# The two layer ends of a hybrid diffusion kernel: result parts by half in one page, places made earlier, sums of squares as columns on TensorE, root and reciprocal ahead of the loop

## The chip, the cores and the metric

One Trainium2 chip, one of its cores. The time is device microseconds of one execution of the whole program; each kernel is run several times, and the median of the runs stands for it.

## The reference

Two layers over 512 token columns (256 of them latent, 256 context) of 1024 channels. Each layer normalises and modulates, mixes with three parts (an S5 scan, an attention with low-rank queries and keys, a Hyena convolution), projects the merged result back, and ends with a mixture of 32 experts of which each token takes two. The second layer needs the latent columns alone. What the change touches is the mixture and the normalisation behind it:

```python
def _rms_norm(x, g):
    xf = x.astype(jnp.float32)
    y = xf * lax.rsqrt(jnp.mean(xf * xf, axis=-1, keepdims=True) + EPS)
    return (y * g.astype(jnp.float32)).astype(x.dtype)

def expert_block(args):                     # inside _hier_moe
    xb, e = args
    return (jax.nn.silu(xb @ w1[e]) * (xb @ w3[e])) @ w2[e]

for i in range(DEPTH):                      # inside reference
    hl = _modulate(xl, norm1_g[i], mod_l[0], mod_l[1])
    ...
    xl = xl + mod_l[2] * (_merge_groups(s5_l, mla_l, hy_l, mix_norm_g[i]) @ w_out[i])
    ...
    y = _hier_moe(fl, moe_w_group[i], moe_w_expert[i], moe_w1[i], moe_w3[i], moe_w2[i])
    xl = xl + mod_l[5] * y.reshape(bsz, n, d)
return _rms_norm(xl, final_g)
```

## The kernel before

The program runs `mixer(0)`, `moe(0)`, `mixer(1)`, `moe(1)` and a final stage (`FIN`), in this order. `xT` holds the running result as eight channel tiles of 128 channels by 512 columns. Weights come in pages of 128x1024 float32 (512 KB) out of a ring of 44 pages, and every one of these transfers is issued by SP, one after another in one fixed order: a page whose place in the ring isn't free yet holds SP until it is, and all that stands behind it in SP's order waits too.

Two things set the order. In `mixer` a scheduler lays out the instructions of every engine by a simulated timeline; in `moe` the order is the written one. Whatever is written between the two calls belongs to the scheduled part.

**The end of `mixer(1)`.** After the last head of the attention (the exponentials on ScalarE, `ACT`, then line 1111 on VectorE, `DVE`, which scales by the reciprocal of the sums in `ATTst`) the output projection (line 1373) runs over eight output tiles m = 0 to 7. Each takes one page of `in_wout`, which ScalarE and VectorE split into a high and a low part first. Pages 0 to 2 are loaded ahead (names `ATTpg<-in_wout`), pages 3 to 7 later (`OUTpg<-in_wout`). Between the two groups SP issues eight pages of the modulation weights (`ADApg<-in_adaw`, used by line 166) and the first 16 expert pages (`ROUTpg<-in_w`). The router follows, then the experts.

**`moe`.** Each of the 32 experts takes twelve pages: eight in `first_half` (line 1582, `pC`, `pY`, `pT` and the like are PSUM banks), then `swiglu`, `turn` (transposes into `hT`), and four in `second_half` (line 1606). `scaled_result` weights the 128 x 512 result, by two halves of 64 rows, and splits it: ScalarE writes the high part into the page `Y[0]`, VectorE (line 1718) the rest into `Y[1]`. A pair of experts shares the 128 rows of these pages. `combine` then spreads the rows back over the columns by a matmul with the 0/1 matrix of places `GT` (lines 1790 and 1868 make it), channel tile by channel tile, and `residual` (line 1620) adds the eight tiles into `xT`. The combines of pair p run during the experts of pair p + 1; those of the last pair stand in `combine_last` (line 1698), where the squares of each finished tile are added up on VectorE (lines 193 and 1709). Layer 0 has one more expert pass, with weights chosen by a register, ahead of `combine_last`. A loop (line 1900) for overfull experts follows; here it runs zero times.

**Behind the loop**, `rstd_of` sums the squares over the channels by matmuls with a column pair of ones (line 201), takes the root on ScalarE (line 118, which needs a table load) and the reciprocal on VectorE (line 205), and spreads it over the partitions by transposes (line 217). In layer 0 this is the start of `mixer(1)`, where four weight pages are split as well (`S5bpg`) before the normalised input is made (line 224, `INPpg`); in layer 1 it is the final stage, which loads the gains `fg` (line 1953, 4 KB) and multiplies (line 1956).

## Time and profile before

| | us |
|---|---|
| runs | 1714.05, 1712.85, 1707.95 |
| median | 1712.85 |
| profiled execution | 1709.9 |
| its span | 1708.1 |
| TensorE busy | 1533.8 (90%) |
| VectorE busy | 888.6 (52%) |
| ScalarE busy | 482.4 (28%) |
| bytes moved | 510.04 MB, mean 299 GB/s |

Some 1.8 us of the profiled execution lie outside its span. Busy shares are means over stages with different limits; which wait ends last in a stage is read from that stage alone.

### The profile page before, as it was taken

The numbers are of one execution on the slowest core, as the hardware profiler recorded it, in microseconds if no ns is written. First come the engines' busy times: TensorE is split into PE (matmuls) and PEld (weight loads), VectorE is DVE, ScalarE is ACT, GpSimd is POOL, SyncE is SP. The second block draws the span as 40 slices with busy tenths as digits, with TensorE's granted clock in tenths as the row PEclk, the third lists the DMA queues.
The fourth block names the chain that finished last, engine by engine and source line by source line (L and its number), as shares of the span: only waits on it lengthen the run. The fifth ranks groups of instructions, "written<-read, shape, count | busy, mean of one in ns | idle before, by whom it ended". The sixth has DMA issues, their size and how long they took to land. (4 is left out here: it accounts for less than half of the span.)

```text
span 1708.1 us, 22533 instructions
## 1 busy us (share of the span) xinstructions
PE 1533.8 (90%) x8073; PEld 788.0 (46%) x8073; DVE 888.6 (52%) x2176; ACT 482.4 (28%) x931; POOL 94.7 (6%) x154
## 2 busy tenths in 40 slices
PE   5888889998999999999899597899799999999995
PEld 1676744476433333344233387547534444333322
DVE  6769565545244546864643758455524434333333
ACT  3343544342111121112122534444311111111112
POOL 0000212003000000002000000010100000000000
PEclk9998899998999999999999698998899999999998
DMA  9111244559999999999999112577799999999994
GB/s 343 64 38 62 79 181 162 218 198 351 374 392 407 409 409 409 409 408 372 373 402 409 61 62 99 205 264 267 293 359 409 409 409 409 409 409 409 409 409 184
DMA packets 143300, 510.04 MB, mean 299 GB/s; under 512 B 17995, under 2 KB 18573, under 8 KB 142929
## 3 DMA queue, kind: packets, MB, share of 16 engines
q1 hardware_dynamic: 138736, 495.21, 75.0%
q0 software_dynamic: 4160, 12.82, 2.2%
q8 instruction: 66, 1.08, 0.3%
q10 hardware_dynamic: 288, 0.52, 0.1%
q14 instruction: 50, 0.40, 0.1%
HBM read 504.85 MB, written 3.64 MB: 298 GB/s over the span
## 5 line engine op out<-in xcount | busy, mean ns | idle before, releaser
L1582 PE MATMUL MOEp<-MOEpg,MOEpg 128*64 128x512 f32 x956 | 227.4, 603 | 13.1 <-DMA MOEpg<-in_w 11.9
L1582 PE MATMUL MOEp<-MOEpg,ROUTpg 128*64 128x512 f32 x960 | 220.5, 603 | 8.2 <-DMA MOEpg<-in_w 7.9
L1718 DVE SCALAR_TENSOR_TENSOR MOEpg<-MOEpY,MOEwt,MOEpg 64x512 fp32r<-64x512 f32 x128 | 96.0, 750 | 241.5 <-ACT MOEpg L118 241.4
L1606 PE MATMUL MOEpY<-MOEpg,MOEhT 128*64 128x512 f32 x960 | 219.4, 599 | 1.8 <-DVE MOEhT L1598 1.8
L1620 DVE SCALAR_TENSOR_TENSOR zxT<-MOEpC,zmod,zxT 128x256 f32<-128x256 f32 x385 | 168.2, 479 | 8.2 <-PE MOEpC L1698 2.1
L118 ACT ACTIVATE MOEpg<-MOEpY,MOEwt 64x512 fp32r<-64x512 f32 x128 | 87.3, 682 | 276.3 <-PE MOEpY L1606 212.2
L1588 DVE TENSOR_TENSOR MOEh<-MOEh,MOEp 128x256 f32<-128x256 f32 x65 | 27.3, 420 | 241.9 <-ACT MOEh L118 241.9
L118 ACT ACTIVATE MOEh<-MOEp 128x256 f32<-128x256 f32 x65 | 24.9, 383 | 399.7 <-PE MOEp L1582 399.7
L1688 PE MATMUL MOEpC<-MOEGT,MOEpg 128*128 128x512 f32 (+1 forms) x496 | 130.0, 364 | 6.7 <-DVE zxT L1620 6.0
L1582 PEld LDWEIGHTS MOEp<-MOEpg,ROUTpg 128*64 128x64 f32 x960 | 64.2, 137 | 149.4 <-issue 103.7
L1582 PEld LDWEIGHTS MOEp<-MOEpg,MOEpg 128*64 128x64 f32 x956 | 59.4, 136 | 159.3 <-DMA MOEpg<-in_w 90.5
L1606 PEld LDWEIGHTS MOEpY<-MOEpg,MOEhT 128*64 128x64 f32 x960 | 63.5, 136 | 120.6 <-issue 93.8
L1688 PEld LDWEIGHTS MOEpC<-MOEGT,MOEpg 128*128 128x128 f32 x496 | 75.2, 189 | 61.7 <-issue 26.8
L166 PE MATMUL ADAb<-ADApg,zcact 128*32 128x512 f32 x384 | 76.1, 614 | 12.8 <-DMA ADApg<-in_adaw 12.8
L788 PE MATMUL PROJb<-INPpg,PROJpg 128*128 128x512 f32 (+1 forms) x384 | 73.8, 356 | 6.4 <-DVE PROJpg L974 5.7
L788 PEld LDWEIGHTS PROJb<-INPpg,PROJpg 128*128 128x128 f32 x384 | 63.5, 206 | 15.9 <-ACT PROJpg L118 6.7
L118 ACT ACT_TABLE_LOAD x35 | 44.9, 1283 | 15.7 <-DVE ATTst L1102 5.7
L1657 PE MATMUL MOEpG<-MOEpg,ROUTpg 128*128 128x256 f32 x240 | 44.7, 310 | 1.1 <-DVE MOEpg L1493 1.1
L1657 PEld LDWEIGHTS MOEpG<-MOEpg,ROUTpg 128*128 128x128 f32 x240 | 33.0, 194 | 24.2 <-issue 15.8
L1091 PE MATMUL ATTb<-QKVpg,QKVpg 96*128 96x512 f32 x64 | 35.4, 654 | 7.3 <-ACT ATTpg L118 7.3
L1373 PE MATMUL OUTb<-OUTpg,ATTpg 128*128 128x512 f32 (+1 forms) x192 | 41.3, 380 | 0.0
L1373 PEld LDWEIGHTS OUTb<-OUTpg,ATTpg 128*128 128x128 f32 x192 | 34.9, 214 | 5.3 <-DVE ATTpg L230 0.2
(541 smaller groups left out, 2115.2 us busy)
## 6 DMA issues: line engine op xcount, KB each, us to landing
MOEpg<-in_w SPq DMA_DIRECT2D x719, 512.0 KB
ADApg<-in_adaw SPq DMA_DIRECT2D x96, 512.0 KB
ROUTpg<-in_w SPq DMA_DIRECT2D x61, 512.0 KB
PROJpg<-in_win SPq DMA_DIRECT2D x16, 512.0 KB
ATTpg<-in_wout SPq DMA_DIRECT2D x8, 512.0 KB
OUTpg<-in_wout SPq DMA_DIRECT2D x8, 512.0 KB
QKVpg<-in_uq SPq DMA_DIRECT2D x5, 512.0 KB
MOEpg<-in_win SPq DMA_DIRECT2D x5, 512.0 KB
```

What stands on the lines that cost most here:

```text
L118: nc.scalar.activation(out, in_, f, **kw)
L166: nc.tensor.matmul(b[q:q + 32, :], cact[:, k, :], w[:, h * 512:(h + 1) * 512], start=(k < 2), stop=(k >= KD - 2), tile_position=(0, q))
L788: nc.tensor.matmul(b, a_[:, c], b_[k][:, c0:], start=(first and n == 0), stop=(last and n == 2))
L1091: nc.tensor.matmul(b, qc[h][:, nq - NS + qt * 128:nq - NS + (qt + 1) * 128], kc[h], start=True, stop=True)
L1373: nc.tensor.matmul(b, a_[:, c], y_, start=(n == 0 and j == 0), stop=(n == KD - 1 and j == 2))
L1582: nc.tensor.matmul(b[64 * h:64 * h + 64, :], X[:, k, :], w[:, h * 512:(h + 1) * 512], start=(k == 0), stop=(k == KD - 1), tile_position=(0 ...
L1588: nc.vector.tensor_mul(h_, h_, b[:, 256:512])
L1606: nc.tensor.matmul(b[64 * h:64 * h + 64, :], hT[:, k % 2, (k // 2) * 64:(k // 2) * 64 + 64], w[:, h * 512:(h + 1) * 512], start=(k == 0), ...
L1620: nc.vector.scalar_tensor_tensor(xT[:, k, seg(s)], b[:, s * NS - c0:(s + 1) * NS - c0], mod[:, 40 + k, s:s + 1], xT[:, k, seg(s)], op0=OP. ...
L1657: nc.tensor.matmul(b[:, kk * 256:(kk + 1) * 256], hs[t][:, k * 128:(k + 1) * 128], G[:, t].rearrange("p e c -> p (e c)"), start=(t == 0 an ...
L1688: nc.tensor.matmul(b, Y_[p][j][rows, k * 128:(k + 1) * 128], GT_[p][rows], start=(j == 0), stop=(j == 1))
L1718: nc.vector.scalar_tensor_tensor(Y[1][rows_of, h * 512:(h + 1) * 512], b[rows], wt[rows], yh.bitcast(F32), op0=OP.mult, op1=OP.subtract)
```

## The change

- `scaled_result` puts both parts of one half of the result in one page (`Y[h]`: high in columns 0 to 511, low in 512 to 1023), and `combine` reads them there through `part_of`.
- `GT` is made ahead of `second_half` instead of behind `scaled_result`; likewise in the extra pass (`extra_places`).
- In layer 1's last expert the four combines that used to stand around `turn` and behind the result now stand inside `first_half`, one ahead of each second page.
- `combine_last` hands the squares to TensorE as column sums (`sum_columns`) while it still combines: three sums in layer 0 (tiles 0 to 5, 6, 7) and five in layer 1 (0+1, 2+3, 4+5, 6, 7). Root and reciprocal (`rstd_from`) come ahead of the loop, and only the spreading (`spread`) behind it.
- The loop's own ring of pages has two instead of four.
- `fg` is loaded between `mixer(1)` and `moe(1)`, in a pool that is opened there and stays open; the final products go into two pages.

```diff
+        for j, sq in enumerate(acc):
+            sum_columns(sq, n, b, j == 0, j == len(acc) - 1)
+        return rstd_from(b, nch, n)
+
+    def sum_columns(sq, n, b, first, last):
+
         nt = n // 128
-        for j, sq in enumerate(acc):
-            for t in range(nt):
-                nc.tensor.matmul(b[:, 2 * t:2 * t + 2], sq[:, t * 128:(t + 1) * 128], ones2,
-                                 start=(j == 0 and t == 0), stop=(j == len(acc) - 1 and t == nt - 1))
-        r = cpool.tile([128, 4], F32, name=uid("rs"), tag="rs", bufs=4)
+        for t in range(nt):
+            nc.tensor.matmul(b[:, 2 * t:2 * t + 2], sq[:, t * 128:(t + 1) * 128], ones2,
+                             start=(first and t == 0), stop=(last and t == nt - 1))
+
+    def rstd_from(b, nch, n, r=None):
+        nt = n // 128
+        if r is None:
+            r = cpool.tile([128, 4], F32, name=uid("rs"), tag="rs", bufs=4)
...
-            rstd1 = rstd_of(None, D, acc=acc)
+            rstd1 = spread(acc, NT)
...
+        def part_of(p, j, k):
+            return Y_[p][k // 4][:, j * 512 + k % 4 * 128:j * 512 + (k % 4 + 1) * 128]
+
         def combine_last(p, rows=slice(0, 128)):
 
-            acc, tags = [], (("pC", 2), ("pC", 2), ("pG", 2 - (i == 0)), ("pY", 1), ("p13", 1 + i))
-            for k in range(KD + 2):
+            tags = (("pC", 2), ("pC", 2), ("pG", 2 - (i == 0)), ("pY", 1), ("p13", 1 + i))
+            total = pb("pT")
+            alone = (5, 6, 7) if i == 0 else (1, 3, 5, 6, 7)
+            sq, ready, first = None, [], True
+            for k in range(KD + 3):
                 if k < KD:
                     b = pb(*tags[k % 5])[:, 0:n]
                     for j in range(2):
-                        nc.tensor.matmul(b, Y_[p][j][rows, k * 128:(k + 1) * 128], GT_[p][rows], start=(j == 0), stop=(j == 1))
+                        nc.tensor.matmul(b, part_of(p, j, k)[rows], GT_[p][rows], start=(j == 0), stop=(j == 1))
                     if k in (0, 2, 4):
                         o = squares()[:, 0:n]
                         for s in range(s0, 2):
...
                         nc.gpsimd.tensor_add(xT[:, k, c0:], xT[:, k, c0:], o)
                     else:
                         residual(b, k)
-                if k > 1:
-                    add_square(acc, xT[:, k - 2, c0:], squares)
-            nc.vector.tensor_add(acc[0], acc[0], acc.pop())
-            return acc
+                for sq_ in ready:
+                    sum_columns(sq_, n, total, first, k == KD + 2)
+                    first = False
+                ready = []
+                if 1 < k < KD + 2:
+                    o = squares()[:, 0:n]
+                    act(o, xT[:, k - 2, c0:], AF.Square)
+                    if sq is not None:
+                        nc.vector.tensor_add(o, o, sq)
+                    sq = None if k - 2 in alone else o
+                    if k - 2 in alone:
+                        ready.append(o)
+            return total
 
         def scaled_result(Y, b, wt, rows_of):
...
-                yh = Y[0][rows_of, h * 512:(h + 1) * 512]
+                yh = Y[h][rows_of, 0:512]
                 act(yh, b[rows], AF.Copy, scale=wt[rows])
-                nc.vector.scalar_tensor_tensor(Y[1][rows_of, h * 512:(h + 1) * 512], b[rows], wt[rows], yh.bitcast(F32),
+                nc.vector.scalar_tensor_tensor(Y[h][rows_of, 512:1024], b[rows], wt[rows], yh.bitcast(F32),
...
+        def extra_places(inf1):
             GT_[-1] = wk([128, n], "GT", 2, F32R)
             nc.vector.tensor_scalar(GT_[-1][0:CAP], iotaN[0:CAP, 0:n], inf1[0:CAP, 0:1], None, op0=OP.is_equal)
...
+                end = i and e == NE - 1
...
-                b = first_half(X, pages, (lambda k: gather(0, k // 2 + 1) if k in (2, 4) else None) if i and e == 0 else None)
+                b = first_half(X, pages, (lambda k: gather(0, k // 2 + 1) if k in (2, 4) else None) if i and e == 0 else (lambda k: combine(p - 1, [4 + k // 2]) if k % 2 else None) if end else None)
...
-                if p:
+                if p and not end:
...
+                idx, wt = info_[p]
+                if r == 1:
+                    GT_[p] = wk([128, n], "GT", 2, F32R)
+                    nc.vector.tensor_scalar(GT_[p], iotaN[:, 0:n], idx, None, op0=OP.is_equal)
                 b = second_half(hT, pages)
...
-            acc = combine_last(-1, slice(0, CAP)) if i == 0 else combine_last(last)
+            total = combine_last(-1, slice(0, CAP)) if i == 0 else combine_last(last)
+            acc = rstd_from(total, D, n)
...
-            ring = [page() for _ in range(4)]
+            ring = [page() for _ in range(2)]
...
+        else:
+            fin = ctx.enter_context(tc.tile_pool(name="fin", bufs=1))
+            fg = fin.tile([128, KD], F32, name="fg", tag="fg")
+            nc.sync.dma_start(fg, A["fg"])
         acc = moe(i, *m)
     stage[0] = "FIN"
-    with tc.tile_pool(name="fin", bufs=1) as fin, tc.tile_pool(name="fp", bufs=1, space=bass.MemoryType.PSUM) as PS[0]:
-        r = rstd_of(None, D, NS, acc=acc)
-        fg = fin.tile([128, KD], F32, name="fg", tag="fg")
-        nc.sync.dma_start(fg, A["fg"])
-        o = fin.tile([128, KD, NS], F32, name="fo", tag="fo")
-        for k in range(KD):
-            nc.vector.scalar_tensor_tensor(o[:, k], xT[:, k, NS:], fg[:, k:k + 1], r, op0=OP.mult, op1=OP.mult)
-            if k in FIN:
-                f = k + 1 - FIN[k]
-                (nc.sync if k % 4 == 1 else nc.scalar).dma_start(A["out"][:, f:k + 1], o[:, f:k + 1])
+    PS[0] = ctx.enter_context(tc.tile_pool(name="fp", bufs=1, space=bass.MemoryType.PSUM))
+    r = spread(acc, NS)
+    o4 = [page().rearrange("p (k c) -> p k c", k=4) for _ in range(2)]
+    for k in range(KD):
+        nc.vector.scalar_tensor_tensor(o4[k // 4][:, k % 4], xT[:, k, NS:], fg[:, k:k + 1], r, op0=OP.mult, op1=OP.mult)
+        if k in FIN:
+            f = k + 1 - FIN[k]
+            (nc.sync if k % 4 == 1 else nc.scalar).dma_start(A["out"][:, f:k + 1], o4[k // 4][:, f % 4:k % 4 + 1])
```

**SP in layer 1, at the end of the attention** (`in_router`: router weights, `in_wout`: output projection, `in_adaw`: modulation weights; each row ends with the semaphores it waits for). Before:

```order
L660 DMA ROUTpg_8745<-in_router 128x288 [waits DMAHW2_49,PE_49]
L114 DMA ATTpg_8903<-in_wout 128x1024 [waits DMAHW3_49,PE_49]
L114 DMA ATTpg_8909<-in_wout 128x1024 [waits DMAHW4_49,DVE_49]
L114 DMA ATTpg_8915<-in_wout 128x1024 [waits DMAHW5_49,PE_49]
L114 DMA ADApg_8946<-in_adaw 128x1024 [waits DMAHW6_49,PE_49]
L114 DMA ADApg_8948<-in_adaw 128x1024 [waits DVE_49,DMAHW7_49,Activation_49,Pool_49]
```

After:

```order
L672 DMA ROUTpg_8777<-in_router 128x288 [waits DMAHW2_49,PE_49]
L1985 DMA fg<-in_fg 128x8 [waits DMAHW3_49,DVE_49,Activation_49]
L114 DMA ATTpg_8935<-in_wout 128x1024 [waits DMAHW4_49,PE_49]
L114 DMA ATTpg_8941<-in_wout 128x1024 [waits DMAHW5_49]
L114 DMA ATTpg_8947<-in_wout 128x1024 [waits DMAHW6_49,PE_49]
L114 DMA ADApg_8978<-in_adaw 128x1024 [waits DMAHW7_49,PE_49]
L114 DMA ADApg_8980<-in_adaw 128x1024 [waits DMAHW0_49,Pool_49]
```

The load of `fg` stands between the router's weights and the pages of the output projection, and it waits for VectorE and ScalarE: its place in SBUF was that of `ATTst`, and what it waits for are the last exponential and the last product of line 1111 of the attention (line 1111 has another number after the change).

**ScalarE behind the loop of layer 0** (`MOErs`: root of the mean square, `S5bpg<-MOEpg`: the four splits). Before:

```order
L1900 REGISTER_ALU
L1900 COMPARE_AND_BRANCH
L1900 UNCONDITIONAL_BRANCH
L118 ACT_TABLE_LOAD
L118 ACTIVATE S5bpg_7242<-MOEpg_6930 128x1024
L118 ACTIVATE S5bpg_7246<-MOEpg_6932 128x1024
L118 ACT_TABLE_LOAD
L118 ACTIVATE MOErs_7234<-MOEb_7229,zeps_78 128x4
L118 ACTIVATE S5bpg_7250<-MOEpg_6934 128x1024
L118 ACTIVATE S5bpg_7254<-MOEpg_6936 128x1024
```

After:

```order
L118 ACT_TABLE_LOAD
L118 ACTIVATE MOErs_7033<-MOEpT_7218,zeps_78 128x4
L1932 REGISTER_ALU
L1932 COMPARE_AND_BRANCH
L1932 UNCONDITIONAL_BRANCH
L118 ACTIVATE S5bpg_7274<-MOEpg_6932 128x1024
L118 ACTIVATE S5bpg_7278<-MOEpg_6934 128x1024
L118 ACTIVATE S5bpg_7282<-MOEpg_6936 128x1024
L118 ACTIVATE S5bpg_7286<-MOEpg_6938 128x1024
```

The root and its table load stand ahead of the loop's branch, and the four splits follow it in a row.

**PE in `first_half` of layer 1's last expert** (`MOEp`: its result, `MOEpC`: a combine). Before, its last four pages and what follows:

```order
L1582 MATMUL MOEp_2707_12492<-MOEpg_12348,MOEpg_11892 64x512 x2
L1582 MATMUL MOEp_2707_12492<-MOEpg_12366,MOEpg_11892 64x512 x2
L1582 MATMUL MOEp_2707_12492<-MOEpg_12371,MOEpg_11892 64x512 x2
L1582 MATMUL MOEp_2707_12492<-MOEpg_12375,MOEpg_11892 64x512 x2
L1688 MATMUL MOEpC_12513<-MOEGT_12434,MOEpg_12352 128x256
L1688 MATMUL MOEpC_12513<-MOEGT_12434,MOEpg_12353 128x256
L1597 MATMUL MOEpT_12518<-zident_66,MOEh_12509 128x128 x2
L1688 MATMUL MOEpC_12522<-MOEGT_12434,MOEpg_12352 128x256
```

After, its first pages:

```order
L1594 MATMUL MOEp_2706_12529<-MOEpg_12352,MOEpg_11929 64x512 x2
L1700 MATMUL MOEpC_12532<-MOEGT_12450,MOEpg_12390 128x256 x2
L1594 MATMUL MOEp_2706_12529<-MOEpg_12373,MOEpg_11929 64x512 x2
L1594 MATMUL MOEp_2706_12529<-MOEpg_12377,MOEpg_11929 64x512 x2
L1700 MATMUL MOEpC_12540<-MOEGT_12450,MOEpg_12390 128x256 x2
L1594 MATMUL MOEp_2706_12529<-MOEpg_12381,MOEpg_11929 64x512 x2
L1594 MATMUL MOEp_2706_12529<-MOEpg_12385,MOEpg_11929 64x512 x2
L1700 MATMUL MOEpC_12548<-MOEGT_12450,MOEpg_12390 128x256 x2
```

Four combines stand between the pages of the last `first_half`, the first of them after one page.

## Rows read from the trace of the kernel before

**Rows 1.** Timeline of PE at the last page of layer 1: start, length, instruction, idle before.

```profile
1679.20 1.08 PE L1582 MATMUL MOEp<-MOEpg,MOEpg 128*64 128x512 f32 x4 [0.20 <-DMA MOEpg<-in_w]
```

**Rows 2.** Stretches: length, busy us of PE, PEld, DVE, ACT, POOL, PEclk, DMA share, GB/s.

```profile
960.00:970.00 10.00, 2.98 (x12) 2.50 (x12) 6.04 (x8) 6.75 (x8) 0.00 (x0) 0.50 0.15 34
...
970.00:980.00 10.00, 8.09 (x23) 5.98 (x24) 10.00 (x26) 6.82 (x16) 0.00 (x0) 0.61 0.22 72
...
1225.00:1245.00 20.00, 17.76 (x84) 7.67 (x84) 6.32 (x26) 4.66 (x11) 0.00 (x0) 0.91 0.56 196
...
1660.00:1670.00 10.00, 8.59 (x38) 2.62 (x38) 1.63 (x4) 0.38 (x1) 0.00 (x0) 1.00 1.03 410
```

**Rows 3.** Timeline of SP in layer 1: start of issue, length of issuing, what is issued.

```profile
1122.05 0.33 SPq L660 DMA_DIRECT2D ROUTpg<-in_router  x1
...
1131.84 4.49 SPq L114 DMA_DIRECT2D ATTpg<-in_wout  x3
...
1137.59 6.97 SPq L114 DMA_DIRECT2D ADApg<-in_adaw  x8
...
1145.23 24.18 SPq L114 DMA_DIRECT2D ROUTpg<-in_w  x16
...
1170.38 16.50 SPq L114 DMA_DIRECT2D OUTpg<-in_wout  x5
```

**Rows 4.** Timeline of DVE, last head of layer 1 attention (L1111 scales by the softmax sums).

```profile
1164.04 0.88 DVE L1111 TENSOR_SCALAR ATTpg<-ATTpg,ATTst 128x512 f32<-128x512 f32 x2
```

**Rows 5.** Timeline of ACT, DVE and PE from the output projection to the first expert.

```profile
1178.28 1.06 ACT L118 ACTIVATE OUTpg<-OUTpg 128x1024 fp32r<-128x1024 f32 x1 [1.96 <-DMA OUTpg<-in_wout]
...
1185.59 1.22 DVE L230 TENSOR_TENSOR OUTpg<-OUTpg,OUTpg 128x1024 fp32r<-128x1024 f32 x1
...
1188.32 1.92 PE L166 MATMUL ADAb<-ADApg,zcact 128*32 128x512 f32 x16
...
1190.17 0.51 PE L1373 MATMUL OUTb<-OUTpg,OUTpg 128*128 128x256 f32 x2
...
1203.78 2.88 PE L1373 MATMUL OUTb<-OUTpg,OUTpg 128*128 128x256 f32 x22
...
1223.39 1.97 PE L1582 MATMUL MOEp<-ROUTpg,MOEpg 128*64 128x512 f32 x8
```

**Rows 6.** Waits of SP from 1224 to 1250 us: total, times, longest.

```profile
SPq L114 <- PE MOEp L1582: 11.5, 13, 5.6
```

**Rows 7.** Timeline of DVE, ACT and PE at the end of layer 0.

```profile
947.32 0.48 DVE L1790 TENSOR_SCALAR MOEGT<-ziotaN,MOEinf 64x512 fp32r<-64x512 f32 x1
...
960.07 0.69 DVE L1709 TENSOR_TENSOR MOEpg<-MOEpg,MOEpg 128x512 f32<-128x512 f32 x1
...
967.19 2.36 DVE L230 TENSOR_TENSOR S5bpg<-MOEpg,S5bpg 128x1024 fp32r<-128x1024 f32 x2 [0.77 <-ACT S5bpg L118]
...
969.46 1.65 DVE L224 SCALAR_TENSOR_TENSOR INPpg<-zxT,zA,MOEb 128x256 f32<-128x256 f32 x4
...
961.34 1.28 ACT L118 ACT_TABLE_LOAD   x1 [2.90 <-DVEq L1900]
...
961.68 1.87 PE L201 MATMUL MOEb<-zones,MOEpg 128*128 128x2 f32 x8 [6.40 <-DVEq L1900]
```

**Rows 8.** Timeline of DVE and PE at the end of layer 1.

```profile
1673.53 0.88 DVE L1620 SCALAR_TENSOR_TENSOR zxT<-MOEpC,zmod,zxT 128x256 f32<-128x256 f32 x2
...
1682.38 0.06 DVE L1899 MEMSET MOEk<- 128x1 f32 x1 [0.82 <-ACT MOEk L118]
...
1697.58 0.42 DVE L1709 TENSOR_TENSOR MOEpg<-MOEpg,MOEpg 128x256 f32<-128x256 f32 x1
...
1690.88 0.99 PE L1698 MATMUL MOEpC<-MOEGT,MOEpg 128*128 128x256 f32 x4 [3.66 <-DVE MOEGT L1868]
...
1700.53 0.69 PE L217 MATMUL FINb<-zident,FINrs 128*128 128x128 f32 x2 [0.56 <-DVE FINrs L205]
```

**Rows 9.** Costliest groups: line, engine, operation, count, busy us, mean ns, idle before and releaser.

```profile
L1718 DVE SCALAR_TENSOR_TENSOR MOEpg<-MOEpY,MOEwt,MOEpg 64x512 fp32r<-64x512 f32 x128 | 96.0, 750 | 241.5 <-ACT MOEpg L118 241.4
```

More of the change, by code (lines that the diff above doesn't have):

```diff
@@ L213, in rstd_of, with spread @@
                 add_square(acc, t, half)
-        r = rstd_columns(acc, nch, n, bank(side=side))
+        return spread(rstd_columns(acc, nch, n, bank(side=side)), n, side)
+    def spread(r, n, side=False):
         b = bank(n=n, side=side)
@@ L1697, in combine_last @@
                     for j in range(2):
-                        nc.tensor.matmul(b, Y_[p][j][rows, k * 128:(k + 1) * 128], GT_[p][rows], start=(j == 0), stop=(j == 1))
+                        nc.tensor.matmul(b, part_of(p, j, k)[rows], GT_[p][rows], start=(j == 0), stop=(j == 1))
                     if k in (0, 2, 4):
@@ L1849, in moe @@
                     gather(q + 1, r4, (1,))
-                if p:
+                if p and not end:
                     combine(p - 1, [4 * r + 1 if i else 4 * r + 2])
@@ L1863, in moe @@
                     fetch(rows_in[r4 // 2], info_[2 * q + 2 + r4 // 2][0])
-                if p:
+                if p and not end:
                     combine(p - 1, range(4 * r + (2 if i else 3), 4 * r + 4))
-                if r == 1:
-                    GT_[p] = wk([128, n], "GT", 2, F32R)
-                    nc.vector.tensor_scalar(GT_[p], iotaN[:, 0:n], idx, None, op0=OP.is_equal)
                 if e >= NAHEAD:
@@ L1916, in moe @@
             turn(h_, hT)
+            extra_places(inf1)
             extra_result(second_half(hT, w), inf1)
@@ L1919, in moe @@
             sq = page()[:, 0:n]
+            total = pb("pT")
             for k in range(KD):
-                act(sq if k else acc[0], xT[:, k, c0:], AF.Square)
-                if k:
-                    nc.vector.tensor_add(acc[0], acc[0], sq)
+                act(sq, xT[:, k, c0:], AF.Square)
+                sum_columns(sq, n, total, k == 0, k == KD - 1)
+            rstd_from(total, D, n, acc)
         mctx.close()
```

6 lines of the change are left out of this document (3 added, 3 removed).

## The prediction

> **What bounds the kernel now.** I read the last stage first. In layer 1's last `first_half` each page's matmuls take 1.08 us and are preceded by a wait for the page itself, to the last one at 1679.20 [rows 1]; in the table by stretch the DMA share there is 1.03 and the rate 410 GB/s [rows 2]. So the experts' stage is bound by the stream of pages, 512 KB each, 1.28 us a page at 410 GB/s, and a shorter chain inside an expert is worth nothing there. At the start of that stage it is otherwise: from 1225 to 1245 the DMA share is only 0.56 [rows 2], and 11.5 us of that time SP waits for matmuls to set a page free [rows 6]. The ring is full; TensorE's start, and not the transfers, then sets when the stream may go on. A delay of that start therefore moves the end of the program by its full length. Outside the experts' stages the layer ends are chains of short operations in which every engine waits for another: TensorE was busy 2.98 of 10 us behind layer 0's loop, at a granted clock of 0.50 (of its two levels the lower, 1.2 GHz) [rows 2].
>
> **Transfers of layer 1: the new place of `fg`.** This is the only edit that reaches outside the layer ends, and I give it the largest term. Before, SP issued the router weights at 1122.05, three pages of the output projection at 1131.84, eight pages of modulation weights at 1137.59, 16 expert pages from 1145.23 and the next page of the output projection at 1170.38 [rows 3]. In the order after, the 4 KB load of `fg` stands directly behind the router weights, and waits for the last product of line 1111, because it is given the space that this product still reads. That product starts at 1164.04, two pieces of 0.88 [rows 4], so it ends near 1164.9. SP works in order: 27 pages that had been issued from 1131.84 on are queued behind this one wait, and nothing else is.
>
> From about 1165.5 the 27 pages and then the fourth page of the output projection go back to back: 28 x 1.28 = 35.8 us, and with some 2 us from issue to the first landing (an estimate from the 1.96 us wait and the rate around it in [rows 5]) the fourth page is there at about 1203.4. ScalarE splits it in 1.06 and VectorE in 1.22 [rows 5]: 1205.5. Before, the split began at 1178.28 and TensorE reached this page only at 1190.17, since the early tiles and the modulation matmuls (to 1190.24) were in front [rows 5]: a cover of about 10 us, which is used up. The term is 1205.5 - 1190.2 = **+15.3 us**. The early tiles m = 0 to 2 lose little: their three pages are the first behind `fg`, landing by 1171.3, some 3 us later than they were used.
>
> TensorE would stand idle for some 12 us in front of that page. What this costs afterwards I take from the row behind layer 0's loop, where after such a stretch the mean clock from 970 to 980 was 0.61 [rows 2]: at the two levels 0.5 and 1.0 that is 7.8 us of 10 at the lower one; TensorE was busy in 8.09 of the 10, so in some 5.9 of the 7.8, and half of that is lost, **+2.9 us**. Bounds: 0, if the clock stays, and 16.5, if all of the rest of the projection (1190.17 to 1206.66 [rows 5]) ran at half speed.
>
> What follows this point keeps its length: from 1190.17 to the first expert matmul at 1223.39 [rows 5] the router's chain is untouched, and behind it the ring is full.
>
> **End of layer 0.** Removed: the 0.48 us of `GT` ahead of the first combine [rows 7], two of seven adds, and behind the loop two table loads of 1.28 us, the sums (1.87 us for 8 matmuls) [rows 7] and the root. Added ahead of the loop: 24 matmuls of the kind that took 0.234 each, 5.6 us at that low clock or about 2.8 at the high one. The first third can't start before the chain of adds is through with tile 5, which is `GT`'s 0.48 and two adds of 0.69 before the last add of before (ended 960.76 [rows 7]), 958.9; so they end near 964.5, or 961.7 at the high clock. Root and reciprocal, about half a us by what they add between the sums and the transposes, bring it to 965.0. Behind the loop (0.6 us, as between 960.76 and 961.34 [rows 7]) the four splits now come in a row: 1.05 on ScalarE, then 4 x 1.18 on VectorE [rows 7], and line 224 follows at about 971.4. It started at 969.46 [rows 7]. The clock was 0.50 there and nothing in the change makes that stretch dense, so I take **+1.9 us**; the other bound is -0.9.
>
> The Trainium skill ("ScalarE: Activation LUTs", section "What ACT_TABLE_LOAD costs") puts a table switch at 1283 ns plus about 1380 ns of draining. By that the two loads removed would be worth 2 x 2.66 us and this term would be -0.9 as well. The trace agrees with the first figure and shows no drain: the load at 961.34 ends at 962.62, and ScalarE's next instruction starts at 962.63.
>
> **End of layer 1.** Three changes meet. The first of the four combines moved into `first_half` needs a PSUM bank that the residual at 1673.53 (two, to about 1674.05) sets free [rows 8], so TensorE, which has the second page by then, stands until 1674.05. Seven pages at no more than 1.08 [rows 1] are left; the combines lie in the overlap of these modelled ends. That is 1681.6, where before the last page ended at 1680.28, so +1.3, and the table load behind it, which the memset at 1682.38 and with it `hT` wait for [rows 8], moves as much. Against that, the first combine of `combine_last` waits no more for the second half of the result (a piece on ScalarE and one on VectorE of 0.75 [rows 9], some 1.5), a residual pair (0.88 [rows 8]) and `GT` (under the 0.48 of layer 0); it began at 1690.88, released by `GT` [rows 8]. 1.3 - 1.5 - 0.9 - 0.4 makes it start 1.5 us earlier. In `combine_last` the sums stand between combines, which holds tiles 5 to 7 by up to 1.5; behind it the last adds to 1698.00 shorten by 0.4 to 1.5, and the sums, root and table load between 1698.00 and the transposes at 1700.53 [rows 8] are mostly gone. Together between -2.7 (high clock) and +1.0 (all at the low clock); I take **-1.3 us**, between them.
>
> **Edits at nothing.** Result parts by half: both pieces of line 1718 still alternate with ScalarE over the same PSUM bank, so the chain in `scaled_result` keeps its length (VectorE waits 241.4 us for ScalarE in these pieces over the program [rows 9]); in the middle of the stage the wait for pages covers it [rows 1]. `GT` earlier, there too. The loop's pages: it runs zero times. `fg` at the end: its load wasn't waited for before.
>
> **The sum.** 15.3 + 2.9 + 1.9 - 1.3 = +18.8 us; on the profiled execution of 1709.9 that is 1728.7. The median of the runs is 2.95 above that execution and would give 1731.7. I forecast **1730 us**, between the two, its own range 1721.5 to 1737.
>
> **Rivals.**
> - **The transfers have room.** SP's wait is real, but the pages come in time: 1711 us (the two ends alone, +0.6). It decides at the fourth page: if it lands by about 1188 no term is left, for which the wait would have to end near 1150 instead of 1165. Speaking for it: from 1225 on the transfers do have slack. Against it: 28 pages need 35.8 us at the full rate whatever comes later, and [rows 4] fixes the start. Or the load of `fg` doesn't wait as the order says. Together 0.13.
> - **Half of it is made up.** The slack of 1225 to 1245 is 44% of 20 us, 8.8 us. If the ring weren't full then, this much would come back: 1721. Against it: SP's waits for matmuls [rows 6]. Chance 0.06.
> - **Every lost transfer counts.** Between 1131.84 and 1165.5 SP issued about 21 pages (3, 8 and some 10 of the 16). If the stream never catches up any of it, 21 x 1.28 = 26.9 us: 1737. It would need a DMA share near 1 from 1205 to 1245 in the profile after. Chance 0.07.
> - **The clock stays low over the rest of the projection**: 16.5 instead of 2.9, 1742. In [rows 2] it came back within the same 10 us. Chance 0.03.
> - **The rate.** As a mechanism here, pages that need 1.46 us instead of 1.28 put the fourth page 5.2 us later: 1734. Against it: 410 GB/s in [rows 2]. Chance 0.01. The Trainium skill ("DMA: Bandwidth & Descriptors", section "Specifications") states 358 GB/s as a core's share of HBM, which is this case; the trace's 410 GB/s speaks against it here.
> - **Both ends gain and nothing else happens**: -0.9 and -2.7, 1706 from the profiled execution, still within 0.5%. To be faster by more, something I don't see is needed: 0.03.
>
> **Chances.** Forecast 0.67, rivals as above. A measurement of this kernel can tell about 0.5%, 8.6 us, from no change, so slower begins at 1721.4. Slower by more: 0.67 + 0.07 + 0.03 + 0.01 + half of the partial case, 0.81; within: 0.16; faster: 0.03. The range for 8 in 10 takes the forecast's own range, the partial case and most of the third rival: 1717 to 1738.
>
> **What would show it.** Right: SP's timeline after shows nothing between the router weights and about 1165, then `in_wout`, `in_adaw` and `in_w` in a row; TensorE waits for the split of an `OUTpg` page until about 1205; the first expert matmul of layer 1 comes some 17 us later and the last one as well. Layer 0's end: no table load behind the loop, line 224 about 2 us later. Layer 1: the last page's matmuls 1 us behind their landing, the transposes 1 us nearer to them. Wrong: the projection's fourth page in place by 1190, or a first expert that is late while the last page isn't.

## The result: 1.5% slower, most of it in front of layer 1's experts

The kernel after takes 1736.10 us (median of 6 runs, 1734.03 to 1740.35), the one before 1709.89 beside it (6 runs, 1707.01 to 1714.05): the ratio is 1.0152, 95% interval 1.0132 to 1.0171. 1730 was forecast, in a range of 1717 to 1738. The profiled execution of after took 1734.03, 24.1 more than the 1709.9 of before. These are the same places in the two traces:

| place | before | after | later by |
|---|---|---|---|
| layer 0: last `second_half` begins | 940.64 | 942.17 | 1.5 |
| layer 0's end: line 224 (236 after) begins | 969.46 | 974.62 | 5.2 |
| last head of the attention: line 1111 (1123 after) begins | 1164.04 | 1165.26 | 1.2 |
| fourth page of the projection, first matmul | 1190.17 | 1207.73 | 17.6 |
| layer 1's first expert, first matmul | 1223.39 | 1244.48 | 21.1 |
| layer 1's last `second_half` begins | 1682.91 | 1706.57 | 23.7 |
| final transposes | 1700.53 | 1724.78 | 24.2 |

Two executions of one kernel differ at such places by some us: the runs of before spread over 7 us. What is read here are differences over short stretches, and beside them medians of several runs. Short stretches vary as well: of the 5.2 us at layer 0's end 1.2 are left at line 1111, so the trace of after takes 3.9 less than that of before between the two places (190.6 and 194.6); but two traces of one and the same kernel, `e4` below, take 194.2 and 191.2 there. These 3.9 us are therefore not put down to the change.

**SP, layer 1, after** (timeline as in [rows 3]; then its waits, total, times, longest, from 1120 to 1170 and from 1245 to 1272):

```profile
1126.08 0.33 SPq L672 DMA_DIRECT2D ROUTpg<-in_router  x1
...
1166.23 0.33 SPq L1985 DMA_DIRECT2D fg<-in_fg  x1
...
1166.66 1.32 SPq L114 DMA_DIRECT2D ATTpg<-in_wout  x3
...
1174.58 20.90 SPq L114 DMA_DIRECT2D ROUTpg<-in_w  x16
...
1196.44 5.43 SPq L114 DMA_DIRECT2D OUTpg<-in_wout  x5
```

```profile
SPq L1985 <- DVE ATTpg L1123: 39.7, 1, 39.7
...
SPq L114 <- PE MOEp L1594: 12.0, 13, 5.6
```

Against [rows 3], nothing is issued between the router weights and 1166.23. The load of `fg` waits 39.7 us for line 1123, which is line 1111 of before, and the 27 pages follow in one go. The second wait answers to [rows 6]: 12.0 us in 13 waits with a longest of 5.6, where before had 11.5, 13 and 5.6. As before, the ring is full when the experts start.

**ScalarE, VectorE and TensorE at the projection's fourth page, and the stretches around it, after** (columns of the second fence as in [rows 2]):

```profile
1206.62 1.06 ACT L118 ACTIVATE OUTpg<-OUTpg 128x1024 fp32r<-128x1024 f32 x1 [29.08 <-DMA OUTpg<-in_wout]
...
1207.71 1.23 DVE L242 TENSOR_TENSOR OUTpg<-OUTpg,OUTpg 128x1024 fp32r<-128x1024 f32 x1 [19.82 <-ACT OUTpg L118]
...
1207.73 0.80 PE L1385 MATMUL OUTb<-OUTpg,OUTpg 128*128 128x256 f32 x2 [14.44 <-ACT OUTpg L118]
...
1208.99 4.96 PE L1385 MATMUL OUTb<-OUTpg,OUTpg 128*128 128x256 f32 x22
...
1244.48 1.94 PE L1594 MATMUL MOEp<-ROUTpg,MOEpg 128*64 128x512 f32 x8
```

```profile
1194.00:1207.00 13.00, 0.00 (x0) 0.00 (x0) 0.00 (x0) 0.38 (x1) 0.00 (x0) 0.60 1.03 409
...
1207.00:1217.00 10.00, 9.19 (x53) 8.70 (x54) 5.16 (x7) 7.19 (x13) 0.00 (x0) 0.67 1.02 399
...
1245.00:1265.00 20.00, 17.76 (x86) 7.74 (x84) 6.25 (x27) 4.20 (x10) 0.00 (x0) 0.91 0.54 185
```

The split of the fourth page waits 29.08 us for its transfer, where [rows 5] had 1.96. While it waits the transfers run at 409 GB/s, and TensorE does nothing from 1194 to 1207. The first two matmuls need ScalarE's part of the split alone. The 22 behind them start 1.26 us later, when VectorE's part is done (1208.94), where before only 0.38 lay between; and they take 4.96 instead of 2.87, at a granted clock of 0.67 from 1207 to 1217. Before, they were:

```profile
1190.55 2.87 PE L1373 MATMUL OUTb<-OUTpg,OUTpg 128*128 128x256 f32 x22
```

From 1245 on, with the experts, the DMA share is 0.54, as [rows 2] had 0.56 from 1225.

**End of layer 0, after** (DVE, PE, ACT; answers to [rows 7]):

```profile
960.59 0.67 DVE L1733 TENSOR_TENSOR MOEpg<-MOEpg,MOEpg 128x512 f32<-128x512 f32 x1
...
974.62 0.47 DVE L236 SCALAR_TENSOR_TENSOR INPpg<-zxT,zA,MOEb 128x256 f32<-128x256 f32 x1
...
961.32 5.28 PE L206 MATMUL MOEpT<-zones,MOEpg 128*128 128x2 f32 x24 [4.49 <-DVE MOEpg L1733]
...
966.63 0.26 ACT L118 ACTIVATE MOErs<-MOEpT,zeps 128x4 f32<-128x4 f32 x1 [5.31 <-PE MOEpT L206]
...
968.99 3.90 ACT L118 ACTIVATE S5bpg<-MOEpg 128x1024 fp32r<-128x1024 f32 x4 [2.09 <-issue]
```

The last add ends at 961.26, all 24 column sums (5.28 us) stand behind it, then root and reciprocal. ScalarE's next instruction comes 2.10 us behind the root, and the profile names nothing that it waits for ("issue").

**End of layer 1, after** (PE, DVE; answers to [rows 1] and [rows 8]):

```profile
1695.56 0.47 PE L1700 MATMUL MOEpC<-MOEGT,MOEpg 128*128 128x256 f32 x2 [2.00 <-DVE zxT L1632]
...
1702.87 1.08 PE L1594 MATMUL MOEp<-MOEpg,MOEpg 128*64 128x512 f32 x4
...
1706.57 3.65 PE L1618 MATMUL MOEpY<-MOEpg,MOEhT 128*64 128x512 f32 x16 [1.25 <-DVE MOEhT L1610]
...
1711.01 0.39 PE L1716 MATMUL MOEpC<-MOEGT,MOEpg 128*128 128x256 f32 x1 [0.78 <-ACT MOEpg L118]
...
1719.91 2.72 PE L206 MATMUL MOEpT<-zones,MOEpg 128*128 128x2 f32 x12 [0.91 <-DVE MOEpg L1733]
...
1724.78 0.69 PE L229 MATMUL FINb<-zident,MOErs 128*128 128x128 f32 x2 [2.15 <-issue]
...
1694.93 0.88 DVE L1632 SCALAR_TENSOR_TENSOR zxT<-MOEpC,zmod,zxT 128x256 f32<-128x256 f32 x2
```

The first moved combine waits for VectorE (the residual pair at 1694.93, which had to wait for the result's second half). The last page's matmuls begin 7.3 us behind that combine, and no wait for their transfer is shown, as there is in [rows 1]. The last 12 records of column sums (2.72) stand in a row behind the last residual, and the transposes follow 2.15 us behind them with nothing but "issue" between.

### The profile page after: what moved, and what is told of

It reads as the page before. It is cut to its first block, busy times and chain, and to the rows that moved or that the text cites. A ratio compares the mean times of both kernels' runs of the same rounds, so it can differ in the third digit from the quotient of the medians.

```text
span 1732.3 us, 22641 instructions
## 1 busy us (share of the span) xinstructions
PE 1542.4 (89%) x8105; PEld 795.3 (46%) x8105; DVE 885.1 (51%) x2170; ACT 478.5 (28%) x928; POOL 94.6 (5%) x154
## 5 line engine op out<-in xcount | busy, mean ns | idle before, releaser
L1385 PE MATMUL OUTb<-OUTpg,OUTpg 128*128 128x256 f32 (+1 forms) x192 | 35.5, 345 | 14.5 <-ACT OUTpg L118 14.4
L1669 PEld LDWEIGHTS MOEpG<-MOEpg,ROUTpg 128*128 128x128 f32 x240 | 33.0, 194 | 24.2 <-issue 17.4
L118 ACT ACT_TABLE_LOAD x32 | 41.1, 1283 | 10.6 <-DVE ATTst L1114 5.7
```

The source lines that it names most:

```text
L118: nc.scalar.activation(out, in_, f, **kw)
L1385: nc.tensor.matmul(b, a_[:, c], y_, start=(n == 0 and j == 0), stop=(n == KD - 1 and j == 2))
L1669: nc.tensor.matmul(b[:, kk * 256:(kk + 1) * 256], hs[t][:, k * 128:(k + 1) * 128], G[:, t].rearrange("p e c -> p (e c)"), start=(t == 0 an ...
```

## Experiments

Theory A: the wait of `fg`'s load, and the pages behind it on SP, cost about 20 us, and the rest of the change a few us at the layer ends. Its rival, theory B: the stream of pages makes the wait good, and the ends cost the time. In all variants but `e2` and `e5`, `fg` lies in the space of the condition vector `cT`, which is read only at the start of the program.

### The change without its wait

```diff
-            fin = ctx.enter_context(tc.tile_pool(name="fin", bufs=1))
-            fg = fin.tile([128, KD], F32, name="fg", tag="fg")
             nc.sync.dma_start(fg, A["fg"])
...
+    fg = cT.rearrange("p a b -> p (a b)")[:, 0:KD]
```

> The changed kernel, with the gains fg loaded into the space of the condition vector cT, which is read only at the start; the load then stands in layer 0 in SP's order and waits for nothing that is late. All else as in the change. Theory A (SP's wait for the space of fg is the cost; in the traces TensorE reached the fourth page of the projection 17.6 us later, 1.2 of it older, then 3.0 at a lower clock and some 1 to 2 on the way to the experts): about 20.5 us less than after, 1715.5, between 1713 and 1718. Theory B (the stream of pages makes the wait good, and the layer ends cost the time): 1733 to 1736. The fourth page's split near 1180 by A, near 1206 by B.

1719.66 us (6 runs), 1.0052 of before (1.0032 to 1.0073): 16.4 less than after, somewhat above the expected span. ACT and PE at the fourth page:

```profile
1183.10 1.06 ACT L118 ACTIVATE OUTpg<-OUTpg 128x1024 fp32r<-128x1024 f32 x1 [1.29 <-DMA OUTpg<-in_wout]
...
1197.42 0.51 PE L1385 MATMUL OUTb<-OUTpg,OUTpg 128*128 128x256 f32 x2
```

The split is back to a wait of 1.29 for its transfer, and TensorE reaches the page without waiting. Theory A holds; what is left over before, some 9 us, is more than the two traces had shown at the ends (6.4), and the steps further down look for it. (The trace of `e1` is of the slowest of its six runs, 1723.38.)

### The wait alone

```diff
+        else:
+            fin = ctx.enter_context(tc.tile_pool(name="fin", bufs=1))
+            fg = fin.tile([128, KD], F32, name="fg", tag="fg")
+            nc.sync.dma_start(fg, A["fg"])
         acc = moe(i, *m)
```

(in the kernel before, and the load in the final stage taken out)

> The kernel before, with only the load of fg moved between the second mixer and the second mixture, in the space that it has in the change (SP's order then shows it behind the router weights, waiting for the attention's last product). Theory A: the whole of the loss, 1709.9 + 20.5 = 1730, between 1727 and 1733, and SP silent from about 1122 to 1165. Theory B: as before, 1710.

1729.91 us (4 runs), 1.0121 of before (1.0092 to 1.0150), as theory A says and not as B. SP and PE:

```profile
1123.42 0.33 SPq L660 DMA_DIRECT2D ROUTpg<-in_router  x1
...
1163.55 0.33 SPq L1951 DMA_DIRECT2D fg<-in_fg  x1
...
1163.97 1.33 SPq L114 DMA_DIRECT2D ATTpg<-in_wout  x3
...
1204.36 0.80 PE L1373 MATMUL OUTb<-OUTpg,OUTpg 128*128 128x256 f32 x2 [16.72 <-ACT OUTpg L118]
```

From line 1111's last start to the fourth page 41.8 us pass (26.1 before, 42.5 after), on to the first expert 36.6 (33.2 and 36.8), on to the last `second_half` 460.3 (459.5 and 462.1). So one 4 KB load that is moved, with no other edit, costs 19.5 us between the medians, and the experts give none of it back.

### The same wait, on another queue

```diff
-            nc.sync.dma_start(fg, A["fg"])
+            nc.scalar.dma_start(fg, A["fg"])
```

(in the kernel after, `fg` in its space there)

> The change, with the load of fg issued by ScalarE instead of SP: the same space, the same wait, but ahead of ScalarE's copies and not of SP's pages. Theory A (what is queued behind the wait costs, not the wait): as e1, 1716, between 1713 and 1719, ScalarE held under 1 us. Theory D (the space taken from the attention's tile or the small transfer itself holds up the stage): 1736.

1726.07 us (4 runs), 1.0090 of before (1.0066 to 1.0113). Neither theory: 10 less than after, 6.4 more than `e1`. SP, then ScalarE's own queue and its split; then SP's longest wait between 1120 and 1250 (total, times, longest):

```profile
1138.84 4.49 SPq L114 DMA_DIRECT2D ATTpg<-in_wout  x3
...
1144.59 28.12 SPq L114 DMA_DIRECT2D ADApg<-in_adaw  x8
...
1169.19 0.39 ACTq L1985 DMA_DIRECT2D fg<-in_fg  x1
...
1201.55 1.06 ACT L118 ACTIVATE OUTpg<-OUTpg 128x1024 fp32r<-128x1024 f32 x1 [21.04 <-DMA OUTpg<-in_wout]
```

```profile
SPq L114 <- DMA fg<-in_fg: 24.0, 1, 24.0
```

SP now passes the wait, but only for seven pages. The issue of the eight modulation pages lasts 28.12 us instead of 6.97. The built order says why; these are two of the loads there:

```
L1985 DMA fg<-in_fg 128x8 [waits DMAHW3_49,DVE_49,Activation_49]
L114 DMA ADApg_8986<-in_adaw 128x1024 [waits DMAHW3_49,PE_49,Activation_49]
```

In this program every load takes one of eight semaphores in turn (the orders shown with the change run from DMAHW2 to DMAHW7 and on to DMAHW0), and waits for the load that had it last; `fg` on ScalarE's queue still takes the one that the eighth page behind it needs. The trace has this wait: 24.0 us of SP, for the landing of `fg`. So SP stood behind `fg` again, for 20 pages instead of 27, and the fourth page came 34.4 us behind line 1111's last start, where it is 42.5 in after and 26.1 in before. That is a second dose of the same cause: 7 pages fewer, 7 x 1.28 = 9.0 us from that, and 8.0 measured.

### What the ends cost, in steps

From `e4` to `e1` one group of edits is added at a time. `e4` is the kernel before with parts by half, places early and `fg` early. (Its expectation names the moved combines too; in the kernel that ran they stood as before the change, so what is said there of them does not hold, and its difference from `e1` includes them.)

```diff
-                yh = Y[0][rows_of, h * 512:(h + 1) * 512]
+                yh = Y[h][rows_of, 0:512]
...
+                if r == 1:
+                    GT_[p] = wk([128, n], "GT", 2, F32R)
+                    nc.vector.tensor_scalar(GT_[p], iotaN[:, 0:n], idx, None, op0=OP.is_equal)
                 b = second_half(hT, pages)
```

> As e1_fg_early, but squares are summed on VectorE and summed over channels, rooted and inverted behind the loop, as before the change; places early, parts by half and the moved combines as in the change. Theory A with the ends as the two traces show them (layer 0's end 3.6 us longer net, of it the 24 column sums 5.3 us and 2.1 us in which ScalarE takes the loop's branch; layer 1's end about 0.6 longer): 4 to 5 us less than e1, 1710.5, between 1708 and 1713. Theory C (the column sums are free and the moved combines and the rest make up what e1 costs over before): as e1, 1715.5.

1708.50 us (10 runs), 0.9990 of before (0.9978 to 1.0003). DVE at the end of layer 0, last add and line 224:

```profile
957.37 0.69 DVE L1712 TENSOR_TENSOR MOEpg<-MOEpg,MOEpg 128x512 f32<-128x512 f32 x1
...
966.76 1.65 DVE L224 SCALAR_TENSOR_TENSOR INPpg<-zxT,zA,MOEb 128x256 f32<-128x256 f32 x4
```

8.70 us between the last add's end and line 224, as in [rows 7]. Theory C, the time of `e1`, is out; the time lies in the span of theory A, though 11.2 us under `e1` and not 4 to 5, and the moved combines are in that difference.

`e6` adds root, reciprocal and the 8 (layer 1: 4) column sums of the added squares ahead of the loop, with the loop's ring of two pages and the final products in pages:

```diff
             nc.vector.tensor_add(acc[0], acc[0], acc.pop())
-            return acc
+            total = pb("pT")
+            for j, sq in enumerate(acc):
+                sum_columns(sq, n, total, j == 0, j == len(acc) - 1)
+            return total
...
+            acc = rstd_from(total, D, n)
```

> As e3_not_moved, but squares are summed on VectorE as before the change; the 8 (layer 0) and 4 (layer 1) column sums of that one tile, the root and the reciprocal stand ahead of the loop. Against e4 it differs by root and sums ahead of the loop, against e3 by the column sums in place of the adds. Theory H (work right ahead of the loop puts the engine's own way through the branch, 2.1 us in after, behind it): behind layer 0's last add line 224 follows in about 10.1 us instead of 8.7, layer 1's transposes in about 3.2 instead of 2.5; in all 2 us over e4, 1710.5, between 1708.5 and 1713; and 3 to 6 us under e3. Theory I (two table loads fewer is a gain, and the column sums alone cost): 1 to 2.5 us under e4, 1706.5.

1712.83 us (12 runs), 1.0019 of before (1.0006 to 1.0031): theory H, with 4.3 between the medians where 2 were expected. DVE and ACT at the end of layer 0, PE at the final transposes:

```profile
961.29 0.69 DVE L1724 TENSOR_TENSOR MOEpg<-MOEpg,MOEpg 128x512 f32<-128x512 f32 x1
...
971.93 1.65 DVE L236 SCALAR_TENSOR_TENSOR INPpg<-zxT,zA,MOEb 128x256 f32<-128x256 f32 x4
...
963.94 0.26 ACT L118 ACTIVATE MOErs<-MOEpT,zeps 128x4 f32<-128x4 f32 x1 [4.28 <-PE MOEpT L206]
...
966.29 3.90 ACT L118 ACTIVATE S5bpg<-MOEpg 128x1024 fp32r<-128x1024 f32 x4 [2.09 <-issue]
...
1703.23 0.69 PE L229 MATMUL FINb<-zident,MOErs 128*128 128x128 f32 x2 [2.24 <-issue]
```

Though two table loads are gone behind the loop, the last add's end and line 224 are now 9.95 us apart instead of 8.70. ScalarE comes out of the branch 2.09 us behind its root. In layer 1 TensorE comes to the transposes 2.24 us behind the sums; they begin 3.38 us behind the end of the last add (1699.85), where it was 2.53 before. Against the trace of `e4`, layer 0 is 1.9 us longer from its first last combine to line 224 (22.5 and 20.6) and layer 1's end 0.9 (17.7 and 16.8); the rest of the 4.3 isn't seen in these two places.

`e3` replaces the adds by the column sums of the change:

```diff
-                if k > 1:
-                    add_square(acc, xT[:, k - 2, c0:], squares)
+                for sq_ in ready:
+                    sum_columns(sq_, n, total, first, k == KD + 2)
```

> As e1_fg_early, but the four combines of layer 1's last pair but one stand where they stood before the change (around the transposes and behind the result), not inside the last first_half. Theory F (the moved combines cost, because the first needs a bank that VectorE sets free only behind the other half's result; from the last second_half but one to the last it took 20.0 us in e1, 18.3 in after, 16.1 in before): 2 to 4 us less there, of which up to 1 comes back in the chain behind; 1717.5, between 1715 and 1719, and 16.1 for that stretch. Theory G (they take the combines off the end, as is meant): 1 to 2 more than e1, 1721.

1716.26 us (6 runs), 1.0041 of before (1.0026 to 1.0055); 3.4 under `e1`, 3.4 over `e6`. PE in layer 0, then the last page and the last sums of layer 1:

```profile
958.53 5.28 PE L206 MATMUL MOEpT<-zones,MOEpg 128*128 128x2 f32 x24 [4.49 <-DVE MOEpg L1733]
...
1682.47 1.08 PE L1594 MATMUL MOEp<-MOEpg,MOEpg 128*64 128x512 f32 x4 [0.21 <-DMA MOEpg<-in_w]
...
1702.04 2.72 PE L206 MATMUL MOEpT<-zones,MOEpg 128*128 128x2 f32 x12 [0.91 <-DVE MOEpg L1733]
```

From the first last combine of layer 0 to line 224 it is 24.4 us (22.5 in `e6`), from the last `second_half` to the final transposes 20.7 (17.7 in `e6`): 1.9 and 3.0. Five sums that stand in TensorE's order between the combines, and wait there for squares, hold the combines behind them. And the last page waits for its transfer again (0.21): the stretch from the last `second_half` but one to the last is 16.6 us, where `e1` had 20.0. This is as theory F says, though not all of the 3.4 us is the stall: the combine behind it and the eight matmuls that follow took 0.75 and 3.29 in `e1`, at a granted clock of 0.72 from 1681 to 1687, and 0.47 and 1.94 in after, which has the same order and the whole stretch in 18.3. In the program's time theory F is not shown here: the intervals of `e1` and `e3` overlap.

`e9` tests its reason, the bank (part of one line):

```diff
-(lambda k: combine(p - 1, [4 + k // 2]) if k % 2 else None) if end
+(lambda k: combine(p - 1, [k]) if k > 3 else None) if end
```

> As e1_fg_early, but the four moved combines stand ahead of pages 4, 5, 6 and 7 of the last first_half instead of 1, 3, 5 and 7. Theory F (it is the bank, which is free by then): no wait of TensorE for VectorE in that first_half, 16.1 to 16.6 us for that stretch, 2 to 4 us less than e1, 1716.5, between 1714 and 1719. Theory J (TensorE has no room for them between pages anywhere): as e1, 1719.7, and the pages no longer waited for.

1714.98 us (12 runs), 1.0033 of before (1.0022 to 1.0043), 4.7 under `e1`, with intervals that still overlap. PE, and the stretch 1684 to 1688:

```profile
1676.42 0.50 PE L1700 MATMUL MOEpC<-MOEGT,MOEpg 128*128 128x256 f32 x2
...
1681.17 1.08 PE L1594 MATMUL MOEp<-MOEpg,MOEpg 128*64 128x512 f32 x4
...
1684.88 5.35 PE L1618 MATMUL MOEpY<-MOEpg,MOEhT 128*64 128x512 f32 x16 [1.25 <-DVE MOEhT L1610]
```

```profile
1684.00:1688.00 4.00, 3.12 (x8) 0.93 (x10) 0.73 (x3) 0.29 (x1) 0.00 (x0) 0.63 0.09 34
```

No combine waits for VectorE now, and that stretch takes 16.7 us, as theory F says and not as J. The combines fill the gaps in which pages 4 to 7 were waited for. One part wasn't expected by any theory: the last `second_half` took 5.35 us instead of the 3.65 of after, at a granted clock of 0.63 in 1684 to 1688. These runs don't show it to be an effect of the edit: `e1` had 5.35 as well, and `e4_again` below, the same kernel as `e4`, had 5.35 where `e4` had 3.65.

### Versions with what was learned

`e10` is `e4` with the late moved combines of `e9`:

> As e4_old_sums (places early, parts by half, fg early; squares, root and reciprocal as before the change; what its expectation says of moved combines did not hold, they stood as before), now with the four combines of layer 1's last pair but one ahead of pages 4 to 7 of the last first_half, as in e9. Theory F (there they lie in the waits for pages): from the last second_half to the final transposes 1.2 us less than the 16.8 of e4 if the second_half runs at the low clock as it did in e9 (5.35 instead of 3.65), 2.9 less if not; 1706.5, between 1704.5 and 1709. Theory K (no gain, the chain behind the result is bound by ScalarE and VectorE): as e4, 1708.5.

1708.81 us (12 runs), 0.9989 of before (0.9977 to 1.0000). From the last `second_half` to the transposes 16.45 us, with that `second_half` at 5.22: 0.35 less than the 16.80 of `e4`, where 1.2 were expected. What follows the `second_half` is 1.9 shorter (11.2, and 13.15 in `e4`), while the expert before it is 0.6 longer (16.7 and 16.1). In the program's time it is no measurable gain beside `e4` (theory K as far as these runs tell).

`e11` adds one line at the end of the loop's body, which never runs:

```diff
+            act(sq[:, 0:1], epsT, AF.Sqrt)
```

> As e10_late_moved, with one root of a constant at the end of the overflow loop's body, so that the table of the root is in place on both ways out of the loop and no table load stands behind it; root and reciprocal stay behind the loop. Theory L (the loads cost where they stand in the chain, and the branch costs nothing as long as the engine came to it early): layer 0 from the last add to line 224 in about 6.5 us instead of 8.7, layer 1's end as e10; 2 us less than e10, 1704.5, between 1702 and 1707. Theory M (the loads are hidden beside the sums on TensorE and the splits): as e10.

1707.11 us (12 runs), 0.9972 of before (0.9961 to 0.9984), the fastest of all here and faster than both kernels; it is at the upper end of what theory L expected, and 1.7 under `e10`. DVE and ACT at the end of layer 0:

```profile
961.49 0.69 DVE L1712 TENSOR_TENSOR MOEpg<-MOEpg,MOEpg 128x512 f32<-128x512 f32 x1
...
968.68 1.65 DVE L224 SCALAR_TENSOR_TENSOR INPpg<-zxT,zA,MOEb 128x256 f32<-128x256 f32 x4
...
962.77 2.00 ACT L118 ACTIVATE S5bpg<-MOEpg 128x1024 fp32r<-128x1024 f32 x2 [2.91 <-DVEq L1907]
...
965.00 0.26 ACT L118 ACTIVATE MOErs<-MOEb,zeps 128x4 f32<-128x4 f32 x1 [0.23 <-PE MOEb L201]
```

6.50 us from the last add's end to line 224, as theory L says; root and reciprocal stay behind the loop, where ScalarE has long taken its branch. Layer 1's end is as in `e10` (16.58). The two traced executions end within 0.5 us of each other (1709.16 here, 1708.72 in `e10`), so the gain is read from this stretch and from the medians, not from the length of these two.

The kernel of `e4` beside these two:

> The kernel of e4_old_sums once more, beside e10 and e11 on the same chip: 0.998 to 1.000 of before, if places early and parts by half are worth the 1.3 us that the two ends of its trace show (28.3 instead of 28.8 from layer 0's last second_half to line 224, 16.8 instead of 17.6 at layer 1's end).

1710.22 us (12 runs), 0.9990 of before (0.9978 to 1.0001): at most a small gain. The stretches that the expectation goes by did not come back: 28.7 us from layer 0's last `second_half` to line 224, and 18.6 at layer 1's end. PE, the last `second_half` in `e4`, then here:

```profile
1680.68 3.65 PE L1606 MATMUL MOEpY<-MOEpg,MOEhT 128*64 128x512 f32 x16 [1.01 <-DVE MOEhT L1598]
...
1685.39 5.35 PE L1606 MATMUL MOEpY<-MOEpg,MOEhT 128*64 128x512 f32 x16 [1.01 <-DVE MOEhT L1598]
```

It is the same kernel; the granted clock around them was 1.00 (1680 to 1686) and 0.72 (1685 to 1691). So two executions of one kernel can differ by 1.7 us at layer 1's end.

## Why the prediction was right, and where its terms were off

The mechanism forecast for the large term is the one that the runs show. That the time lies inside the range, 1.9 us below its upper end, owes something to the room left for the rivals: the two layer ends were forecast too small, one of them with the wrong sign.

**Transfers: right, by its own steps.** `fg` waits for line 1111, 27 pages wait for `fg`, and the fourth page is what TensorE then waits for. Predicted from the attention's last product (1164.9) to the page's first matmul: 40.6 us. Measured: 1166.2 to 1207.73, 41.5. Two errors in it work against each other: from the first page's issue (1166.66) to the fourth page's split (1206.62) it is 39.96 us, where 2 + 28 x 1.28 = 37.8 had been put down, and the first matmul waited for ScalarE's part of the split alone. VectorE's part, for which the forecast had 1.22, held up the third. +15.3 was forecast and +16.3 came, beside the 1.2 that after was late already. `e1`, `e2` and `e5` bear it out as the cause.

**Clock: right in kind, its size partly luck.** The rest of the projection took 16.5 us before and 19.4 after (1207.73 to 1227.2): +2.9 forecast, +2.9 measured. But only 2.1 of it is the slower run of the 22 matmuls; another 0.9 passed ahead of them (1.26 and 0.38), where they waited for VectorE's part of the split. The mean clock of the ten us from 1207 was 0.67, where the estimate went by 0.61.

**No way back: right.** From the first expert to the last `second_half` but one it is 443.4 us before and 443.8 after, and SP's waits for a free page at the start are the same to half a us. The second rival (8.8 us made up by the ring) falls with this, and so does the third (every lost page counts): SP lost 40 us of issuing and the program 16, and the sign that it named is missing, since the DMA share was 0.42 from 1217 to 1230. The first (the transfers have room) falls with `e2`. The rate held too, 409 GB/s from 1194 to 1207, so that the 358 GB/s of the Trainium skill ("DMA: Bandwidth & Descriptors", section "Specifications") isn't what this stretch shows. That figure is a stack's 716 GB/s divided by two cores, and here one core runs, so it was not "this case", as the prediction has it.

**End of layer 0: right sign, too small.** +1.9 forecast; from the last `second_half` to line 224 it is 28.8 and 32.4, +3.6. Two terms of the sum were mis-sized. The way out of the loop was taken as 0.6 us, from [rows 7], and measured 1.88 (968.99 - 967.11): in before ScalarE had come to the branch early, and waited there for VectorE; with the root ahead of it the engine's own 2.1 us stand behind the root. And the last add came 1.0 us earlier, counted from `second_half`, instead of 1.9. The sums themselves were right (5.6 forecast, 5.28 measured). The Trainium skill's figure for a table switch ("ScalarE: Activation LUTs", section "What ACT_TABLE_LOAD costs": 1283 ns and about 1380 ns of draining) stands against these runs as it stood against [rows 7]: taking two loads out shortened `e11`'s stretch by 2.2 us, under two loads of 1.28, and nowhere near the 5.3 that an estimate from that section gives.

**End of layer 1: wrong sign.** -1.3 forecast; the last expert took 2.2 longer (18.3 instead of 16.1) and the chain from there to the transposes 0.6 (18.2 instead of 17.6), +2.8. The step on the bank was right in kind (the combine waits for exactly that residual), and mis-sized: behind the stall each pair of pages with its combine took 2.30 us, which I had taken as 2.16 with the combine in the overlap. The first combine of `combine_last` came even earlier than forecast, 4.4 us behind the start of `second_half`, where before it was 8.0 and 5.2 follow from the forecast. What failed is the step behind it: "the sums, root and table load [...] are mostly gone". From that combine to the transposes it is 13.8 us instead of 9.7, since TensorE holds its combines for the sums, then runs 12 records in a row (2.72), and comes through the branch 2.15 us later.

**The sum.** 18.8 forecast, 24.1 between the profiled executions, 26.2 between the medians. The ends are the largest error, 6.4 instead of 0.6. With them the four terms as measured come to 25.6; the traces differ by less, since after was 1.5 late ahead of the first end and 3.9 shorter between line 224 and line 1111, with some 1 us spread over the rest. So this one pair of traces doesn't show that layer 0's 3.6 us reach the end of the program; that root and sums ahead of the loop cost time is shown by `e6` over `e4` and `e3` over `e6` (4.3 and 3.4 between the medians), in which both ends are changed. `e1` and `e2`, 0.52% and 1.21% over before, agree with the 1.52% of after within their intervals.

**What stays open.** `e1` is 11.2 us above `e4` in the medians, and the stretches in their two traces make up 10.3: 3.7 in layer 0 (32.0 and 28.3), 3.9 in the last expert (20.0 and 16.1), 2.7 behind it (19.5 and 16.8). The two traced executions are 16.6 apart, though, and 6.7 of that lie ahead of layer 0's last `second_half`, before the places that the edits touch. Of the last two stretches 3.3 us are the level of the clock: 1.6 right behind the stall (18.3 in after, 20.0 in `e1`) and 1.7 in the last `second_half` (3.65 and 5.35). The stall itself costs 2.2 us, as in after. Since `e4` and `e4_again` differ in the same way, these 3.3 us can't be put down to the change, and why the clock falls at these places in one execution and not in the next stays open.

## What to carry to other kernels

Where a load is moved up, look at what its space was used for last, and at everything that stands behind it in the queue: a load that takes 0.3 us to issue can hold a whole stream, and its price is read from the order of the queue and from the first piece of work that runs out of cover. Another issuing engine doesn't free the stream as long as the loads share a turn of semaphores. Work that is moved ahead of a branch to get it off the path behind it puts the engine's own way through the branch onto the path; here it was cheaper to leave the work behind the branch and to make sure that what it needs (here the table) is in place on both ways there. And before a difference of one or two us between two traces is given a cause, a second trace of one of the kernels tells how much of it comes and goes by itself: here 1.7 us at layer 1's end and 3.0 between line 224 and line 1111.

## What the runs showed of the hardware that I had not expected

- An engine whose last work stands right ahead of the loop needs 2.1 to 2.2 us to its next instruction behind it (ScalarE 2.10 in after, 2.09 in `e6`; TensorE 2.15 in after, 2.24 in `e6`). Where it came early, 0.6 us behind VectorE's last add were seen ([rows 7]).
- One and the same `second_half`, the last of layer 1, took 3.65 us in some traces (before, after, `e2`, `e3`, `e4`, `e5`, `e6`) and 5.22 to 5.35 in others (`e1`, `e9`, `e10`, `e11`, `e4_again`), at granted clocks of 1.00 (after, 1706 to 1711) and 0.72 (`e1`, 1694 to 1700). Whether combines fill the gap ahead of it doesn't decide it: after and `e5` have none there and took 3.65, and `e4_again` has them and took 5.35.
